# Modulation vectors: turning the four column quarters' sums with PE transposes and adding them on VectorE, in place of a float32 product with a folding matrix

## The chip, the core and the metric

The kernel runs on one core of one Trainium2 chip. The metric is the device time of one execution in microseconds (us); lower is better. The engines are named as the profile names them: PE is the matrix engine's matmul, PEld its weight load, DVE the vector engine, ACT the scalar engine, POOL the general engine, SP the engine whose queue issues nearly all DMAs.

## The reference, cut to what matters

The reference is one step of a two-layer decoder (layer 0 is RWKV-7, layer 1 sparse attention) for 1024 prompt tokens and for 8 sample sequences of 8 tokens. Every layer begins with its modulation vectors:

```
def ada_mods(c, w, b):
    m = jax.nn.silu(c) @ w + b
    return jnp.split(m[:, None, :], 6, axis=-1)
...
        sh_a, sc_a, g_a, sh_f, sc_f, g_f = ada_mods(c, P['w_ada'][i], P['b_ada'][i])
        h = rms_norm(x, P['norm_g'][i, 0]) * (1 + sc_a) + sh_a
        ...
        x = x + g_a * o
        h = rms_norm(x, P['norm_g'][i, 1]) * (1 + sc_f) + sh_f
        ...
        x = x + g_f * ((u * u) @ P['w_down'][i])
```

`c` has 9 rows (8 sample sequences and 1 prompt) of 1024 numbers, `w_ada[i]` is 1024 by 6144. So each layer turns 9 rows into 6 vectors of 1024 for each row: a product of few rows with a wide matrix. The rest of the step (projections, the RWKV recurrence, the choice of keys, attention, the feed-forward layers) is not touched by the change.

## The kernel before, in words

The activations lie with the 1024 model channels on partitions, as 8 blocks of 128. The large products (`mm3`, L140) split float32 operands into a high and a low part and add three products; their weights come through `loadw`, which splits them on ACT (L122) and on DVE or POOL (L126).

The modulation vectors are made in 24 steps of 256 columns for each of the two layers, 48 in all, by the generator `ada_steps`. `ada_prep` computes SiLU(c), turns it (L235) and keeps it in `cst`, 8 blocks of 128 channels by 32 columns, of which 9 hold rows and the others zero. A step does this:

- two loads of 512 KB of `w_ada` (L261, tile `wa`), each 4 blocks of 128 channels by 256 columns;
- eight float32 products (L264). The block k of a half (k = 0 to 3) writes output partitions 32k to 32k+31, so that the four blocks stand under each other in one PSUM tile `oa`; the second half is added to the first there. Thus `oa` holds four partial sums ("column quarters" of PE), each of 9 rows by 256 columns, at partitions 0, 32, 64 and 96;
- ACT copies `oa` to SBUF (L266, tile `adas`);
- `fold(s, sb)` then adds the four quarters and turns the result, so that the 256 columns come to lie on partitions as the activations' channels do. It is written one step late: the fold of step s-1 stands behind the products and the copy of step s. The product (L250) has the 128 by 128 half of `adas` as its stationary operand and a constant 128 by 10 matrix `fold` as the moving one, which has a 1 at row 32k + r, column r; so one product both turns and adds. DVE then adds the bias `b_ada` and writes the step's two columns of 128 channels by 9 rows into `mods` (L251).

The eight steps that layer 0's first norm needs run first (in `run`, with the load of the first group of tokens among them); `ada_fin` (L276) then makes `gm`, and `rwkv_h` applies `gm` and `mods` (L368, L371, L372). The other 40 steps are taken one at a time between the blocks of the RWKV projections of group A (64 sample columns and 512 prompt columns): `for _ in self.rwkv_proj(GA, hA): next(more, None)`. Those that are then left run one after the other. In this part the tiles `wa` have 3 buffers, the PSUM tiles `oa` and `pa` 2 each, `adas` 2. When the steps are done, their pools are closed, and the RWKV recurrence and group B's work begin.

Each engine works its own queue in order. The order in the queues is laid down when the program is built, and it is not always the order of the text.

Of the kernel before, what the change touches and what calls it, by code (L numbers as in the profile page):

```python
# [9 lines left out]
F32 = mybir.dt.float32  # L10
# [5 lines left out]
ALU = mybir.AluOpType  # L16
# [61 lines left out]
class Kern:  # L78
# [145 lines left out]
    def ada_prep(self):  # L224
        nc, cp = self.nc, self.cp
        c = self.quarter("c9", F32)[0:9].rearrange("p a b -> p (a b)")[:, 0:1024]
        nc.sync.dma_start(c[0:8], self.I["c_sample"])
        nc.sync.dma_start(c[8:9], self.I["c_prompt"])
        th = self.quarter("th9", F32)[0:9].rearrange("p a b -> p (a b)")[:, 0:1024]
        nc.scalar.activation(out=th, in_=c, func=AF.Tanh, scale=0.5)  # L230
        nc.vector.tensor_scalar(out=th, in0=th, scalar1=0.5, scalar2=0.5, op0=ALU.mult, op1=ALU.add)
        nc.vector.tensor_tensor(out=th, in0=th, in1=c, op=ALU.mult)
        o = self.mmt()
        for k in range(8):
            nc.tensor.transpose(o[:, k * 9:k * 9 + 9], th[:, k * 128:k * 128 + 128], self.ident[0:9, 0:9])  # L235
        self.cst = self.adp.tile([128, 8, 32], F32, name="cst")
        nc.vector.memset(self.cst, 0.0)
        nc.vector.tensor_copy(self.cst[:, :, 0:9], o[:, 0:72].rearrange("p (k r) -> p k r", k=8))
        self.mods = [cp.tile([128, 48, 9], F32, name=f"mods{l}") for l in range(2)]
        self.gm = [cp.tile([128, 2, 8, 9], F32, name=f"gm{l}") for l in range(2)]  # L240
        self.fold = self.adp.tile([128, 10], F32, name="fold")
        nc.sync.dma_start(self.fold, self.I["c_fold"])

    def ada_steps(self, l, s0, s1, pools):
        nc = self.nc

        def fold(s, sb):
            p = pools[1].tile([128, 512], F32, name="pa", tag="pa")
            for j in range(2):
                nc.tensor.matmul(p[:, j * 10:j * 10 + 10], sb[:, j * 128:j * 128 + 128], self.fold, start=True, stop=True)  # L250
            nc.vector.tensor_tensor(  # L251
                out=self.mods[l][:, s * 2:s * 2 + 2, :], in0=p[:, 0:20].rearrange("p (j r) -> p j r", j=2)[:, :, 0:9],
                in1=self.bada[:, l * 48 + s * 2:l * 48 + s * 2 + 2].unsqueeze(2).to_broadcast([128, 2, 9]), op=ALU.add)

        last = None
        for s in range(s0, s1):
            yield
            o = pools[1].tile([128, 512], F32, name="oa", tag="oa")
            for hf in range(2):
                w = pools[0].tile([128, 4, 256], F32, name="wa", tag="wa")  # L260
                nc.sync.dma_start(w, self.I["w_ada"][l, hf * 512:hf * 512 + 512, s * 256:s * 256 + 256].rearrange("(k p) f -> p k f", p=128))  # L261

                for k in range(4):
                    nc.tensor.matmul(o[k * 32:k * 32 + 32, 0:256], self.cst[:, hf * 4 + k, :], w[:, k, :], start=(hf == 0), stop=(hf == 1))  # L264
            sb = pools[2].tile([128, 256], F32, name="adas", tag="adas")
            nc.scalar.copy(sb, o[:, 0:256])  # L266
            if last:
                fold(*last)
            last = (s, sb)
        fold(*last)  # L270
# [1391 lines left out]
def consts():  # L1662
    c = {}
    c["c_ident"] = np.eye(128, dtype=np.float32)
    p = np.arange(128)
    s, t = p[:, None] % 64, np.arange(64)[None, :]
    strict, incl = (s < t), (s <= t)
    same = (s // 8) == (t // 8)
    gm = np.zeros((128, 2, 128), np.float16)
    gm[:, 0, :64], gm[:, 0, 64:] = strict, incl  # L1670
    gm[:, 1, :64], gm[:, 1, 64:] = strict & same, incl & same
    c["c_gmask"] = gm
    lm = np.zeros((128, 6, 128), np.float16)
    for i in range(6):
        m = 1 << i
        a, b = p[:, None], p[None, :]
        M = ((a // (2 * m)) == (b // (2 * m))) & ((a // m) % 2 == 1) & ((b // m) % 2 == 0)
        M = M | (a == b)
        lm[:, i, :] = M.T if i == 0 else M
    c["c_lmask"] = np.concatenate([lm[:64, :, :64], lm[64:, :, 64:]])  # L1680
    c["c_bones"] = ((p[:, None] // 64) == (p[None, :] // 64)).astype(np.float32)
    c["c_smask"] = ((p[:, None] % 64) // 8 == np.arange(8)[None, :]).astype(np.float32)
    rm = np.ones((128, 2, 256), np.float16)
    rm[:, 0, ::64] = 0
    rm[:, 1, ::8] = 0
    c["c_rmask"] = rm
    inv = np.float32(500000.0) ** (-np.arange(8, dtype=np.float32) * np.float32(2.0) / np.float32(16))
    rp = np.zeros((128, 9, 16), np.float32)
    for i in range(9):
        pos = (PAST + (p % 8) if i == 0 else (i - 1) * 128 + p).astype(np.float32)  # L1690
        ang = (pos[:, None] * inv[None, :]).astype(np.float32)
        rp[:, i, 0:8], rp[:, i, 8:16] = np.cos(ang), np.sin(ang)
    c["c_rope"] = rp
    c["c_cmask"] = np.where(p[None, :] <= p[:, None], 0, -3.0e38).astype(np.float32)
    c["c_csm"] = np.where(np.arange(8)[None, :] <= (np.arange(64)[:, None] % 8), 0, -3.0e38).astype(np.float32)
    c["c_qmask"] = (np.arange(8)[None, :] == (np.arange(128)[:, None] % 8)).astype(np.float32)
    c["c_iota16"] = (p[:, None] % 16).astype(np.float32)
    f = np.zeros((128, 10), np.float32)
    for r in range(128):
        if r % 32 < 9:  # L1700
            f[r, r % 32] = 1
    c["c_fold"] = f
    return c


# [40 lines left out]
```

## Time and profile before

| | us |
|---|---|
| median of 3 runs | 4280.88 |
| lowest, highest run | 4253.56, 4290.66 |
| profiled execution, its own time | 4286.67 |
| its span, first to last instruction | 4284.8 |
| mean granted PE clock in it | 0.915 of full speed |

The span is the stretch that all rows below are measured in; 1.9 us of the profiled execution's time lie around it. Busy shares are means over the whole span; the change touches only the first tenth of it.

### The profile page before, as it was taken

The numbers are of one execution on the slowest core, as the hardware profiler recorded it, in microseconds if no ns is written. First come the engines' busy times: TensorE is split into PE (matmuls) and PEld (weight loads), VectorE is DVE, ScalarE is ACT, GpSimd is POOL, SyncE is SP. The second block draws the span as 40 slices with busy tenths as digits, with TensorE's granted clock in tenths as the row PEclk, the third lists the DMA queues.
The fourth block names the chain that finished last, engine by engine and source line by source line (L and its number), as shares of the span: only waits on it lengthen the run. The fifth ranks groups of instructions, "written<-read, shape, count | busy, mean of one in ns | idle before, by whom it ended". The sixth has DMA issues, their size and how long they took to land.

```text
span 4284.8 us, 76620 instructions
## 1 busy us (share of the span) xinstructions
PE 3983.1 (93%) x31120; PEld 3196.4 (75%) x31120; DVE 2277.6 (53%) x5534; ACT 1688.9 (39%) x3147; POOL 964.0 (22%) x762
## 2 busy tenths in 40 slices
PE   7998899998999999989799888989988999999999
PEld 5787665666777799989655555778767777988777
DVE  5512775543667533341886954332899854444232
ACT  5632554433445333331454333332443334324332
POOL 1321321311433222212111122222101000222222
PEclk6798787978999999999799999998879999999999
DMA  6676122323322122234332156335211111323332
GB/s 217 203 235 210 51 71 71 95 56 99 111 60 61 46 76 81 83 111 123 118 95 65 50 177 209 120 122 152 91 41 46 45 40 45 118 89 96 94 94 84
DMA packets 555889, 433.84 MB, mean 101 GB/s; under 512 B 93777, under 2 KB 517313, under 8 KB 550354
## 3 DMA queue, kind: packets, MB, share of 16 engines
q1 hardware_dynamic: 549650, 391.20, 30.5%
q0 software_dynamic: 5888, 37.75, 2.5%
q8 instruction: 245, 4.01, 0.4%
q14 instruction: 106, 0.87, 0.1%
HBM read 360.48 MB, written 67.87 MB: 100 GB/s over the span
## 4 chain that ended last, share of the span: by engine, by line
PE 70%; DVE 14%; issue 6%; ACT 3%; DMA 3%; POOL 1%; SPq 0%; DVEq 0%; ACTq 0%; POOLq 0%
PE o L140 42%; DVE tj L1204 3%; PE o L1035 3%; PE po L1299 2%; PE pt L1293 2%; PE sp L1186 1%; PE gp L706 1%; PE tp L733 1%; DMA kvraw<-in_cache_k,ix 1%; PE sp L1185 1%; PE rb L659 1%; POOL wl L126 1%; PE sps L1509 1%; PE tp L754 1%; PE spn L930 1%
## 5 line engine op out<-in xcount | busy, mean ns | idle before, releaser
L126 POOL TENSOR_TENSOR wl<-w,wh 128x1024 fp32r<-128x1024 f32 (+1 forms) x258 | 612.0, 2373 | 2317.3 <-ACT wh L122 2038.6
L140 PE MATMUL o<-hi,wh 128*128 128x512 f32 (+4 forms) x2592 | 882.5, 345 | 21.9 <-ACT hi L144 21.8
L140 PE MATMUL o<-lo,wh 128*128 128x256 f32 (+4 forms) x2592 | 885.9, 343 | 16.4 <-DVE lo L145 11.9
L140 PE MATMUL o<-hi,wl 128*128 128x512 f32 (+4 forms) x2592 | 880.2, 340 | 0.1
L122 ACT CAST wh<-w 128x1024 fp32r<-128x1024 f32 (+3 forms) x388 | 401.3, 1034 | 998.6 <-PE o L140 906.1
L140 PEld LDWEIGHTS o<-hi,wh 128*128 128x128 f32 (+1 forms) x2592 | 498.2, 194 | 75.1 <-ACT hi L144 25.6
L140 PEld LDWEIGHTS o<-lo,wh 128*128 128x128 f32 (+1 forms) x2592 | 499.9, 193 | 70.1 <-DVE lo L145 16.3
L140 PEld LDWEIGHTS o<-hi,wl 128*128 128x128 f32 (+1 forms) x2592 | 498.6, 192 | 48.9 <-issue 11.1
L140 PE MATMUL o<-ul,wh 128*128 128x320 f32 (+2 forms) x1536 | 515.2, 336 | 20.8 <-DVE ul L145 20.7
L140 PE MATMUL o<-uh,wh 128*128 128x320 f32 (+2 forms) x1536 | 511.8, 336 | 2.1 <-DVE tno L1214 1.2
L140 PE MATMUL o<-uh,wl 128*128 128x320 f32 (+2 forms) x1536 | 512.6, 336 | 0.0
L397 DVE SCALAR_TENSOR_TENSOR xr<-o,mods,xr 128x256 f32<-128x256 f32 (+1 forms) x432 | 246.5, 571 | 320.4 <-PE o L140 319.5
L140 PEld LDWEIGHTS o<-ul,wh 128*128 128x128 f32 x1536 | 295.1, 192 | 51.3 <-DVE ul L145 28.3
L140 PEld LDWEIGHTS o<-uh,wh 128*128 128x128 f32 x1536 | 293.4, 192 | 35.1 <-ACT uh L144 8.1
L140 PEld LDWEIGHTS o<-uh,wl 128*128 128x128 f32 x1536 | 295.3, 192 | 25.0 <-issue 5.1
L145 DVE TENSOR_TENSOR ul<-z,uh 128x512 fp32r<-128x512 f32 (+1 forms) x128 | 129.7, 1014 | 319.0 <-ACT uh L144 318.9
L126 DVE TENSOR_TENSOR wl<-w,wh 128x1024 fp32r<-128x1024 f32 (+2 forms) x130 | 161.0, 1238 | 225.2 <-ACT wh L122 223.2
L1035 PE MATMUL o<-wl,hi 128*128 128x256 f32 (+2 forms) x648 | 188.0, 292 | 6.9 <-POOL wl L126 6.9
L1035 PE MATMUL o<-wh,hi 128*128 128x256 f32 (+2 forms) x648 | 187.1, 291 | 6.9 <-ACT hi L144 6.9
L1035 PE MATMUL o<-wh,lo 128*128 128x256 f32 (+2 forms) x648 | 183.9, 291 | 0.0
L1204 DVE TENSOR_SCALAR_CACHE_REDUCE tj<-sc,tcf 128x384 bf16<-128x384 f32 (+2 forms) x192 | 180.7, 941 | 2.8
L1276 ACT ACTIVATE sm<-sm,st 128x128 f32<-128x128 f32 (+7 forms) x128 | 99.3, 775 | 126.6 <-DVE st L1275 79.9
(415 smaller groups left out, 6838.7 us busy)
## 6 DMA issues: line engine op xcount, KB each, us to landing
w<-in_w_up SPq DMA_DIRECT2D x128, 512.0 KB
w<-in_w_down SPq DMA_DIRECT2D x128, 512.0 KB
wa<-in_w_ada SPq DMA_DIRECT2D x96, 512.0 KB
w<-in_rw_w_rkv SPq DMA_DIRECT2D x48, 512.0 KB
w<-in_att_w_in SPq DMA_DIRECT2D x32, 512.0 KB
RA<-pt SPq DMA_DIRECT2D x48, 288.0 KB
RB<-pt SPq DMA_DIRECT2D x48, 256.0 KB
in<-RA SPq DMA_DIRECT2D x32, 320.0 KB
```

Source lines behind the costliest of these rows:

```text
L122: nc.scalar.copy(h[:kp, :n], w[:kp, :n])
L126: eng.tensor_tensor(out=l[:kp, :n], in0=w[:kp, :n], in1=h[:kp, :n], op=ALU.subtract)
L140: nc.tensor.matmul(o[0:M, 0:c1 - c0], a, b[:, c0:c1], start=(i == 0 and q == 0), stop=(i == n - 1 and q == 2))
L145: (lo_eng or self.nc.vector).tensor_tensor(out=lo, in0=src, in1=hi, op=ALU.subtract)
L397: nc.vector.scalar_tensor_tensor(out=xm[:, p0:c1], in0=o[:, p0 - c0:c1 - c0], scalar=self.mods[l][:, j * 8 + m, 8:9], in1=xm[:, p0:c1], op ...
L659: nc.tensor.matmul(ps[half(h), i * n:i * n + n], y(i)[:, h:h + 1].to_broadcast([n, 64]), self.ident[0:n, 0:n], start=True, stop=True)
L706: nc.tensor.matmul(pvs[h][:, c, :], BK[hp, c].rearrange("p b t -> p (b t)")[:, h * 64:h * 64 + 128], AR[hp, c].rearrange("p b t -> p (b t) ...
L1035: nc.tensor.matmul(o[0:n, 0:cw], a, w, start=(k == 0 and q == 0), stop=(k == 7 and q == 2))
L1204: nc.vector.tensor_scalar(out=junk[:, 0:L], in0=s, scalar1=th if isinstance(th, float) else th[:, i:i + 1], scalar2=None, op0=op, op1=ALU. ...
L1276: nc.scalar.activation(out=sm[:, 0:L], in_=sm[:, 0:L], func=AF.Exp, scale=-1.0, bias=mn[:, 0:1], accum_out=sums)
L1293: nc.tensor.transpose(ps[:, jj * 128:jj * 128 + 128], sms[h + p][0][:, (j0 + jj) * 128:(j0 + jj) * 128 + 128], self.ident)
L1299: nc.tensor.matmul(out[gk][half(p), pr], self.V[:, j0 + jj, gk * 64:gk * 64 + 64], PTs[p][:, jj * 128:jj * 128 + 128], start=(j0 + jj == 0 ...
```

## The change

`fold` no longer multiplies with the folding matrix. PE turns each 128 by 128 half of `adas` with the identity that other transposes of the kernel use, into 128 PSUM columns each. A reduction on DVE then reads, for each of the two halves and 9 rows, the four quarters (32 columns apart) and adds them into `mods`. A second DVE instruction adds the bias in place. The constant `c_fold`, its tile and its load go.

```diff
@@ ada_prep
         self.gm = [cp.tile([128, 2, 8, 9], F32, name=f"gm{l}") for l in range(2)]
-        self.fold = self.adp.tile([128, 10], F32, name="fold")
-        nc.sync.dma_start(self.fold, self.I["c_fold"])
@@ ada_steps
         def fold(s, sb):
             p = pools[1].tile([128, 512], F32, name="pa", tag="pa")
             for j in range(2):
-                nc.tensor.matmul(p[:, j * 10:j * 10 + 10], sb[:, j * 128:j * 128 + 128], self.fold, start=True, stop=True)
+                nc.tensor.transpose(p[:, j * 128:j * 128 + 128], sb[:, j * 128:j * 128 + 128], self.ident)
+
+            m = self.mods[l][:, s * 2:s * 2 + 2, :]
+            nc.vector.tensor_reduce(out=m, in_=p[:, 0:256].rearrange("p (j k r) -> p j r k", j=2, k=4)[:, :, 0:9, :], axis=mybir.AxisListType.X, op=ALU.add)
             nc.vector.tensor_tensor(
-                out=self.mods[l][:, s * 2:s * 2 + 2, :], in0=p[:, 0:20].rearrange("p (j r) -> p j r", j=2)[:, :, 0:9],
+                out=m, in0=m,
                 in1=self.bada[:, l * 48 + s * 2:l * 48 + s * 2 + 2].unsqueeze(2).to_broadcast([128, 2, 9]), op=ALU.add)
@@ consts
-    f = np.zeros((128, 10), np.float32)
-    for r in range(128):
-        if r % 32 < 9:
-            f[r, r % 32] = 1
-    c["c_fold"] = f
```

## Rows read from the trace of the kernel before

**Rows 1.** The page: span, and busy time of each engine.
```profile
span 4284.8 us, 76620 instructions
...
PE 3983.1 (93%) x31120; PEld 3196.4 (75%) x31120; DVE 2277.6 (53%) x5534; ACT 1688.9 (39%) x3147; POOL 964.0 (22%) x762
```

**Rows 2.** Stretches of time: us, then busy us (count) of PE, PEld, DVE, ACT, POOL, clock, DMA.
```profile
130.00:152.00 22.00, 18.22 (x124) 14.16 (x124) 20.68 (x26) 17.00 (x31) 10.60 (x6) 0.98 0.60 192
152.00:188.00 36.00, 36.00 (x161) 24.18 (x159) 13.30 (x22) 15.83 (x29) 8.98 (x5) 0.54 0.45 149
...
204.00:247.00 43.00, 42.88 (x364) 38.98 (x363) 3.99 (x9) 13.52 (x26) 9.53 (x4) 1.00 0.86 268
```

**Rows 3.** Line L250, the product with the folding matrix: ns min/median/max, first and last start.
```profile
L250 PEld LDWEIGHTS pa<-fold,adas x192: 186/192/338, 11.3 to 408.6; 128*128 128x128 f32 x192
L250 PE MATMUL pa<-fold,adas x192: 172/258/387, 11.3 to 408.6; 128*128 128x10 f32 x192
```

**Rows 4.** The chain of waits, 0 to 412 us: shares by line, then start, us, what.
```profile
by line: PE o L140 42.3%; PE oa L264 7.0%; PE pa L250 4.0%; DMA wa<-in_w_ada 3.9%; PE o L605 2.4%; DVE xn L533 2.3%; issue 2.3%; ACT wh L122 1.5%; DMA w<-in_rw_w_rkv 0.9%; ACT ks L602 0.8%; DVE lo L145 0.8%; ACT hi L144 0.8%; DVE xn L531 0.
...
107.77 1.00 PE oa L264 x16
108.77 0.54 PE pa L250 x4
...
119.97 1.86 PE oa L264 x16
121.84 0.96 PE pa L250 x4
...
382.14 6.44 PE o L140 x48
...
389.58 0.54 PE pa L250 x4
...
390.97 6.05 DMA wa<-in_w_ada
...
408.06 0.95 PE pa L250 x4
```

**Rows 5.** The timeline of the first eight steps: start, us, engine, line.
```profile
26.58 0.93 PEld L250 LDWEIGHTS pa<-fold,adas 128*128 128x128 f32 x4 [1.35 <-ACT adas L266]
...
48.50 0.93 PEld L250 LDWEIGHTS pa<-fold,adas 128*128 128x128 f32 x4 [1.43 <-ACT adas L266]
...
49.78 0.23 DVE L276 SCALAR_TENSOR_TENSOR gm<-mods,vec 128x72 f32<-128x72 f32 x1
```

**Rows 6.** Transposes with the identity: line L307; runs of them in PE's timeline.
```profile
L307 PE MATMUL o<-c_ident,xr x72: 270/273/328, 3912.3 to 4278.7; 128*128 128x128 f32 x64, 128*64 128x128 f32 x8
...
4275.14 3.85 PE L307 MATMUL o<-c_ident,xr 128*128 128x128 f32 x32
...
410.51 1.97 PE L294 MATMUL o<-c_ident,xin 128*128 128x128 f32 x8
```

**Rows 7.** DVE operations nearest to the two of the change, by their shapes.
```profile
L1076 DVE TENSOR_REDUCE ss<-sq 128x1 f32<-128x64 f32 x8 | 1.7, 211 | 0.6 <-ACT sq L1075 0.6
L238 DVE COPY cst<-o x1: 234/234/234, 8.5 to 8.5; 128x72 f32<-128x72 f32 x1
L251 DVE TENSOR_TENSOR mods<-pa,vec 128x18 f32<-128x18 f32 x48 | 8.4, 175 | 142.4 <-PE pa L250 142.4
```

**Rows 8.** SP's queue near the start; ACT's order at the first steps.
```profile
1.88 0.36 SPq L242 DMA_DIRECT2D fold<-in_c_fold  x1
...
19.86 0.69 ACT L331 ACTIVATE acc<-x 128x576 f32<-128x576 f32 x1
...
23.58 0.37 ACT L266 COPY adas<-oa 128x256 f32<-128x256 f32 x1
```

**Rows 9.** The longest waits of 0 to 410 us: total, times, longest.
```profile
DVE mods L251 <- PE pa L250: 142.4, 40, 10.0
```

**Rows 10.** Transposes of the attention (L1293) in one stretch: busy PE, PEld, clock.
```profile
3500.00:3600.00 100.00, 19.47 (x119) 12.77 (x118) 1.00 0.15 43
```

## The prediction

> **What bounds the kernel now.** I read the page first: PE is busy 93% of a span of 4284.8 us and DVE 53% [rows 1]. That is a mean over stages, so I asked next where the changed lines run. The product with the folding matrix (L250) starts between 11.3 and 408.6 us and never after [rows 3]. The change can act only in the first tenth of the span; whatever it gains there reaches the end as a shift of everything behind it, if nothing behind it stands still.
>
> The table of stretches shows what kind of time that tenth is. In 204 to 247 us PE is busy 42.88 of 43.00 us, at full clock, with DVE nearly idle; in 152 to 188 us it is busy all the time at a granted clock of 0.54, that is mostly at the lower of its two levels; in 130 to 152 us DVE is the engine without a gap (20.68 of 22.00) [rows 2]. So most of the stretch is PE's own time, and a microsecond less of PE work is a microsecond, except around 130 to 152 us, where DVE is late, and where loads are late: the chain of waits has 3.9% of 412 us in loads of `w_ada`, the longest 6.05 us long [rows 4]. The chain gives the folding product 4.0% of 412 us, some 16 us [rows 4]. That is the ceiling for the part after 104 us (the chain cannot be followed further back than that; the first 50 us I read in the timeline).
>
> **The change part by part.**
>
> *PE, removed.* 48 folds of two products gave 192 weight loads and 192 matmuls [rows 3]: every float32 product runs as two pairs. A fold is thus four pairs, each a full 128-column weight load with 10 columns behind it, and the loads set its length: 0.54 us in the chain where the clock is high, 0.96 us where it is low [rows 4].
>
> *PE, added.* The transposes of line L307 are 72 in the text (nine blocks, two halves, four each) and 72 in the trace [rows 6], so a float32 transpose is one pair, not two. The data is again the stationary operand and now 128 identity columns follow instead of 10. At the end of the kernel 32 of them take 3.85 us with the tail of the last one (0.27 us) inside: (3.85 - 0.27) / 31 = 0.115 us apiece; at the low clock 8 take 1.97 us with a tail of 0.33 us (the longest of line L307): (1.97 - 0.33) / 7 = 0.23 us [rows 6]. Two of them: 0.23 us at the high clock, 0.46 us at the low one. A fold saves 0.54 - 0.23 = 0.31 us, or 0.96 - 0.46 = 0.50 us. Bounds: were two transposes as short as one pair of the old fold (0.54 / 4 = 0.13 us), 0.41 us at the high clock; were they to run as two passes each, nothing.
>
> *Where these lie on the path.* (a) The first eight steps: from 26.58 to 48.50 us the timeline has six folds at the low clock, each behind the copy that it or its neighbour waits for and each with PE's next products right behind it [rows 5], and one at the high clock before them: 6 x 0.50 + 0.31 = 3.3 us. The fold at 11.26 us lies ahead of a wait for loads and counts nothing. (b) 104 to 204 us: of the chain's 26 fold pieces two high ones and five low ones lie here, the first at 108.77 and at 121.84 us: 2 x 0.31 + 5 x 0.50 = 3.1 us. A short third piece at 128.41 us ends on DVE and gains nothing, since DVE gets more to do there. (c) 204 to 391 us: 14 whole high pieces, the last at 389.58 us [rows 4], 14 x 0.31 = 4.3 us, and two cut ones, 0.3 us. The folds here that are no pieces of the chain run while ACT prepares the next block, and count nothing. (d) 391 to 412 us: PE waits for loads [rows 4], but the loads are issued when the products behind a fold have freed a buffer, so the chain runs through two low folds, the last at 408.06 us [rows 4]: 1.0 us. Of the folds between 51 and 104 us, which the chain doesn't show, I take none. Sum: 3.3 + 3.1 + 4.6 + 1.0 = 12.0 us.
>
> *DVE, added.* A reduction of 72 numbers from PSUM into 18, and the addition now follows it. The reduction of 64 numbers takes 211 ns and a copy of 72 numbers from PSUM 234 ns; the addition took 175 ns and will again [rows 7]. I take 0.23 us a step, 11 us in all, in a stretch where DVE is idle in most parts: it stood 142.4 us in 40 waits for the fold itself [rows 9], so the reduction begins where that wait ended and the next DVE work is late by 0.25 us at most. What hides this is that DVE is not last; without that cover it is all 11 us. Who waits for `mods`: `gm`, once, after the eighth step [rows 5], and the work behind the last step: 2 x 0.25 = 0.5 us on the path. The chain has no fold in DVE's full stretch (130 to 152 us), only the one just ahead. Bound: were all ten pairs between 104 and 204 us on DVE's path, 2.3 us.
>
> *The constant and its load.* One issue of 0.36 us leaves SP's queue at 1.88 us [rows 8], and all later loads are issued that much sooner. The first thing that PE and ACT wait for is `c`, issued before it, so I count nothing; if the loads of the first steps were the only limit, 0.36 us. PSUM: `pa` keeps its size and its two buffers; 256 of its columns are written instead of 20.
>
> *Sum.* 12.0 - 0.5 = 11.5 us less. Against the profiled execution: 4286.7 - 11.5 = 4275.2 (span 4273.3). That execution lies 5.8 us above the median of the runs, so for a median I take 4280.9 - 11.5 = 4269. The three runs lie 37 us apart, and 1% of the time (43 us) is about what a measurement of this kernel can tell from no change: the forecast is well below that.
>
> **The rivals.**
>
> *Given back.* The time is saved but a later wait takes it: loads of `w_ada` that PE already waits for (the 6.05 us at 390.97, [rows 4]) land when the memory delivers them, not when PE is ready. If all that (b) to (d) gain is lost so, only (a) stays: -3 us, 4278. For it: DMA is busy 0.86 of 204 to 247 us [rows 2]. Against it: in that very stretch PE has no gap, so the loads come in time.
>
> *The queues' order, to the bad.* The order in the queues is not that of the text: ACT's squares of the norm (L331), written behind all eight steps, run at 19.86 us, before the second step's copy at 23.58 [rows 8]. With other instructions the build may lay them otherwise. The place where it would hurt is DVE's queue, which stands at the head of a fold for up to 10.0 us [rows 9]; today this hides, as DVE has nothing urgent behind it. If a pair is laid ahead of the splits that feed PE's next projection, PE stands as long. There are three such changes of projection between 128 and 251 us: 3 x 10 = 30 us, less the 11.5 gained: 4299. It decides as soon as more than 11.5 us of such waits come onto PE's path. For it: nothing in the trace fixes the order. Against: the change alters two instructions of a step, and where it moves queues the waits can as well get shorter.
>
> *The order, to the good.* The same, with waits that go. PE's gap in DVE's full stretch is 22.0 - 18.2 = 3.8 us [rows 2] and the loads' part of the chain is 3.9% of 412, 16 us [rows 4]: all of it and the forecast's 11.5 are 31 us, 4250.
>
> *The clock.* Between the folds of 204 to 391 us the granted clock is full [rows 2]; L264's sixteen pieces take 1.00 us there and 1.86 us at the low level [rows 4]. A transpose that let the clock fall would cost the block behind it: 6.44 us of products [rows 4] would take up to 1.86 times as long, 5.5 us more; on 14 folds 77 us, less 11.5: 4346. The trace speaks against it: in 3500 to 3600 us, 119 transposes lie between products and the granted clock is 1.00 [rows 10]. The Trainium skill (TensorE: Matmul & The Clock Gate, Part 4: PE-mode transpose) speaks against the change here: it says that transposes don't count as busy time in the same way and that the full clock doesn't engage for them. By that rule this rival would be the forecast; the stretch at 3500 us, with its clock of 1.00, doesn't agree with it for transposes mixed with products.
>
> *It doesn't do what it says.* If this transpose runs as two passes, like a product, four pairs with 128 columns replace four with 10: nothing gained, DVE's 0.5 us lost, 4281. Line L307's count speaks against it.
>
> **How the numbers follow.** Forecast 0.56 (its own range 4250 to 4284, from the runs' spread around it); given back 0.14; order to the bad 0.12; order to the good 0.12; clock 0.03; two passes 0.03. The likeliest gives 4269. The range must leave out no more than 2 in 10: it takes in both order rivals, with the runs' spread a little beyond them, 4232 to 4300, and leaves out the clock. Faster by over 1% (under 4238): a third of the good order and a little of the forecast's spread, 0.07; slower by over 1% (over 4324): the clock and the worst of the bad order, 0.05; within 1%: 0.88.
>
> **What would show it.** In the changed kernel's profile: 96 transposes with 96 weight loads in place of 192 and 192; fold pieces of about 0.22 and 0.40 us in the chain; a reduction of some 0.23 us for each step on DVE; `gm` made near 46.7 us rather than 49.78; the last fold near 397 us rather than 408, and everything behind it in the same order and as long as before. Wrong would be: PE's gaps before 412 us grown by more than PE's work shrank (given back), queues in another order with DVE waits on PE's path (order), a lower granted clock in 204 to 391 us (clock), or the time behind 412 us changed by more than a few us, which none of my steps foresees.

## The result, and the profile after

The changed kernel takes 4231.45 us (median of 4 runs, 4227.15 to 4245.93) against 4279.41 us before (4 runs beside it), a ratio of 0.990 with a 95% interval of 0.986 to 0.994. It is faster, by some 43 us by the ratio and 48 us by the medians; the forecast was 11.5 us. (The ratios here leave out runs that lie over 1.5% above their kernel's fastest, so they can differ a little from the medians.) The profiled execution took 4245.93 us, the slowest of the four. In the changed kernel the lines behind `fold` stand one higher than before: L265 is the old L264, and so on.

The operations first. By source line (ns min/median/max, first and last start), the transposes, the reduction, the addition; then the addition by its shape with its mean:

```profile
L248 PEld LDWEIGHTS pa<-c_ident,adas x96: 137/142/230, 11.6 to 391.2; 128*128 128x128 f32 x96
L248 PE MATMUL pa<-c_ident,adas x96: 271/328/477, 11.6 to 391.4; 128*128 128x128 f32 x96
...
L251 DVE TENSOR_REDUCE mods<-pa x48: 217/232/234, 12.3 to 391.8; 128x18 f32<-128x72 f32 x48
L252 DVE TENSOR_TENSOR mods<-mods,vec x48: 158/179/1861, 13.3 to 392.6; 128x18 f32<-128x18 f32 x48
...
L252 DVE TENSOR_TENSOR mods<-mods,vec 128x18 f32<-128x18 f32 x48 | 29.3, 612 | 1.2
```

96 pairs stand where 192 stood [rows 3], and the reduction takes the 0.23 us of the forecast. The addition doesn't take what was forecast: its median is 179 ns, but it now has a mean of 612 ns and a longest of 1861, where the old one had a mean of 175 [rows 7]. The timeline (start, us) shows what it stands beside when it is long:

```profile
201.59 2.40 POOL L126 TENSOR_TENSOR wl<-w,wh 128x1024 fp32r<-128x1024 f32 x1 [5.35 <-PE oa L265]
201.91 0.23 DVE L251 TENSOR_REDUCE mods<-pa 128x18 f32<-128x72 f32 x1 [5.64 <-PE pa L248]
202.18 1.84 DVE L252 TENSOR_TENSOR mods<-mods,vec 128x18 f32<-128x18 f32 x1
```

POOL's split began at 201.59 and ends at 203.99; the addition begins inside it and ends with it, at 204.02. The reduction inside the same split is not stretched. The whole timeline bears this out: 18 of the 48 additions take over 0.3 us, and each of the 18 overlaps an instruction of POOL and ends within 0.04 us of that instruction's end. In the kernel before 25 additions overlap one too, and none takes over 0.18 us:

```profile
L251 DVE TENSOR_TENSOR mods<-pa,vec x48: 164/177/178, 13.3 to 409.0; 128x18 f32<-128x18 f32 x48
```

Now the stages, by the columns of [rows 2]. Before, from `gm` to the steps' last product, and from there to the last L605 (a small product at the end of group B's key projection):

```profile
49.80:406.80 357.00, 332.90 (x2439) 275.99 (x2439) 130.05 (x263) 163.03 (x301) 90.83 (x48) 0.85 0.66 212
406.80:1042.10 635.30, 577.70 (x5935) 393.36 (x5927) 354.27 (x977) 280.77 (x623) 162.99 (x209) 0.78 0.26 71
```

and the same two stretches of the changed kernel, with its 20 to 50 us ahead of them:

```profile
20.00:50.00 30.00, 17.11 (x155) 9.30 (x155) 19.58 (x86) 14.07 (x28) 0.00 (x0) 0.82 0.97 317
...
43.50:389.90 346.40, 318.71 (x2351) 259.39 (x2355) 157.07 (x299) 161.71 (x299) 91.83 (x48) 0.87 0.71 221
389.90:998.50 608.60, 550.27 (x5981) 376.67 (x5973) 356.79 (x984) 281.66 (x626) 163.20 (x209) 0.83 0.27 74
```

So the lead is 6.3 us at `gm` (43.5 against 49.8), 16.9 us at the last product, 43.6 us at the last L605; 34.5 us at the last update of the recurrence's state, 1467.5 against 1502.0, in these rows of the kernel before and of the changed one:

```profile
L921 DVE SCALAR_TENSOR_TENSOR S<-S,EL,spn x128: 268/276/283, 472.3 to 1502.0; 128x64 f32<-128x64 f32 x128
```
```profile
L922 DVE SCALAR_TENSOR_TENSOR S<-S,EL,spn x128: 268/276/282, 450.8 to 1467.5; 128x64 f32<-128x64 f32 x128
```

At the end it is 41.0 us (spans 4284.8 and 4243.8). More than half of the lead is made behind 393 us, where no instruction of the change runs. In that stretch the granted clock is 0.83 instead of 0.78. The granted clock has two levels, 1 and a half, so this is some 0.34 x 609 = 207 us at the low one instead of 0.44 x 635 = 280.

What differs there is the order of the queues. With the steps' own instructions left out, the two built programs have the same instructions, but about one in eight of PE's stands in another order than before. All of these lie behind the steps and before 1500 us; from there on all queues are the same.

### The profile page after: what moved, and what is told of

Its sections match the earlier page's. It is cut to its first block, busy times and chain, and to the rows that moved or that the text cites. A ratio compares the mean times of both kernels' runs of the same rounds, so it can differ in the third digit from the quotient of the medians.

```text
span 4243.8 us, 76490 instructions
## 1 busy us (share of the span) xinstructions
PE 3933.9 (93%) x31024; PEld 3154.4 (74%) x31024; DVE 2310.4 (54%) x5582; ACT 1690.0 (40%) x3147; POOL 963.7 (23%) x762
## 4 chain that ended last, share of the span: by engine, by line
PE 54%; DVE 12%; issue 5%; DMA 2%; ACT 2%; POOL 1%; SPq 0%; DVEq 0%; ACTq 0%; POOLq 0%
PE o L140 34%; DVE tj L1205 4%; PE o L1036 3%; PE po L1300 2%; PE pt L1294 2%; PE sp L1187 1%; DMA kvraw<-in_cache_k,ix 1%; PE sp L1186 1%; POOL wl L126 1%; PE gp L707 1%; DVE ul L145 1%; PE ip L1187 1%; PE sps L1510 1%; PE tp L734 1%; DVE xr L398 1%
## 5 line engine op out<-in xcount | busy, mean ns | idle before, releaser
L140 PE MATMUL o<-hi,wh 128*128 128x256 f32 (+4 forms) x2592 | 883.2, 345 | 18.1 <-ACT hi L144 17.5
L140 PE MATMUL o<-hi,wl 128*128 128x256 f32 (+4 forms) x2592 | 879.8, 340 | 0.7 <-POOL wl L126 0.7
L140 PE MATMUL o<-ul,wh 128*128 128x320 f32 (+2 forms) x1536 | 513.4, 335 | 20.9 <-DVE ul L145 20.7
```

The lines of the kernel that those rows point to most:

```text
L140: nc.tensor.matmul(o[0:M, 0:c1 - c0], a, b[:, c0:c1], start=(i == 0 and q == 0), stop=(i == n - 1 and q == 2))
```

## Experiments

Twelve measurements were made, of eleven kernels, each beside the kernel before. Two theories were to be told apart. *Theory W*: the shorter folds, and what they do to PE's clock, give the gain. *Theory O*: half comes from the queues' other order, which the build lays down when the steps at the end have other instructions. In the built programs the order behind 412 us depends on the last steps alone: if the last eight steps of layer 1 are the old ones, it is the order of before, whatever the 40 others are, and if they are the new ones, it is that of the changed kernel. PE's queue, the steps left out, is exactly one of the two in seven of the eleven programs, and differs from one of them in fewer than ten places in the other four. That gives each order with either kind of fold. Within theory W two readings are kept apart: *theory P*, that a fold's number of pairs and their length count, and *theory C*, that the transposes' 128 columns bring PE's clock up by themselves. In the edits below, words in capitals stand for code that is cut short. Each `gm`, last product and last L605 is that of one profiled execution, set against the one profile of the kernel before; that execution (4286.7 us) is some 16 us longer than the medians of the later runs of the same kernel (4269.7 to 4270.9), so the differences of whole times decide.

**40 new folds, old order** (`last8_old`). `fold` is written with both ways, chosen by step:

```diff
-            for j in range(2): OLD PRODUCT
+            new = not (l == 1 and s >= 16)
+            for j in range(2): TRANSPOSE if new else OLD PRODUCT
+            if new: REDUCE
+            ADD BIAS IN PLACE if new else OLD ADDITION
```

> 40 of the 48 steps fold by transposes, the last eight of layer 1 by the old product. The queues behind 412 us are then laid as in the kernel before. Theory W (the shorter folds and PE's clock before 412 us give the gain, which is then only carried to the end): nearly the whole gain stays, 35 to 43 us under before, the last fold some 15 us sooner than 408 us, and the lead grows behind it as in the changed kernel. Theory O (some 15 us are gained before 412 us and the rest by the other order of the queues between 412 and 1500 us): the last fold is some 15 us sooner, the lead stays at that size to the end, 12 to 20 us under before.

Measured: 4242.0 us (median of the ten runs that the ratio keeps; 4245.5 of all twelve) against 4270.1, -28.1 us, 0.992 (0.988 to 0.996). Its stretches from `gm` and from the last product:

```profile
44.60:374.50 329.90, 299.23 (x2375) 247.10 (x2377) 157.05 (x295) 160.90 (x301) 90.80 (x48) 0.94 0.72 230
374.50:1029.70 655.20, 595.96 (x5934) 404.75 (x5927) 355.48 (x977) 282.02 (x623) 163.71 (x209) 0.76 0.25 68
```

The lead of this execution is 32.3 us at the last product and only 12.4 us at the last L605: against the kernel before the clock was higher in the first stretch (0.94 and 0.85) and lower in the second (0.76 and 0.78). The runs' -28.1 lies between the two theories, so by itself it settles nothing.

**8 new folds, new order** (`last8_new`). The same with `new = l == 1 and s >= 16`.

> Only the last eight steps of layer 1 fold by transposes, the 40 others by the old product. The queues behind 412 us are then laid as in the changed kernel. Theory W: next to nothing of the work is changed, 0 to 6 us under before. Theory O: little before 412 us (0 to 4 us), then a lead of 17 us or more that appears between 412 and 1500 us, 15 to 28 us under before in all.

Measured: 4246.2 us against 4270.1, -23.9 us, 0.996 (0.993 to 0.998).

```profile
50.90:401.90 351.00, 325.19 (x2418) 267.57 (x2418) 131.11 (x269) 161.62 (x299) 90.80 (x48) 0.87 0.68 215
401.90:999.70 597.80, 538.16 (x5980) 368.34 (x5973) 356.14 (x984) 281.58 (x626) 162.96 (x209) 0.85 0.27 75
```

With 40 of 48 folds as before, the lead is 4.9 us at the last product and 42.4 us at the last L605. The runs' 23.9 us (18 by the ratio) is theory O's number and not W's (0 to 6 us): the order alone is worth some 20 us. The lead of 42.4 us in this one profile is no proof of it, as the next experiment but one shows.

**Only the first eight steps new** (`first8_new`; `new = l == 0 and s < 8`), order of before.

> Only the eight first steps of layer 0 fold by transposes; the order of all queues but for four DVE instructions is that of before. If the transposes themselves bring PE's clock up in the first 50 us (theory C), the factors gm are ready near 43.5 us as in the changed kernel, at a granted clock over 0.8 in 20 to 50 us. If the clock's rise there was chance, gm is ready near 46.7 us with the shorter folds alone, at a clock near 0.58. Whole time 3 to 7 us under before, or the same within its interval.

Measured: 4263.6 us against 4270.1, -6.5 us, 1.000 (0.997 to 1.003): the same. `gm` came at 43.6 us in the profile, at a clock of 0.82 in 20 to 50 us, as theory C says. One execution was not enough for that, as the next but one shows. In this profile the last product came at 385.4 us, 21.4 us sooner than before's, with eight folds of 48 changed and no gain that the runs show. So the time of the last product in one profile doesn't measure the folds either.

```profile
385.40:1011.50 626.10, 567.49 (x5935) 387.89 (x5927) 353.80 (x977) 280.38 (x623) 163.05 (x209) 0.80 0.26 72
```

**One pass, 10 columns** (`one_pass`). The tiles `adas` and `fold` become fp32r, with a cast of the matrix (`fold`'s lines are left out here); order of before.

```diff
-            sb = pools[2].tile([128, 256], F32, name="adas", tag="adas")
+            sb = pools[2].tile([128, 256], F32R, name="adas", tag="adas")
```

> The old product with 10 columns, but in the reduced float32 form (fp32r) of the large products: the sums and the folding matrix are rounded to it, so that a fold needs two pairs instead of four, with one DVE instruction as before and the order of before. If fewer pairs are what pays, it is as good before 412 us as the transposes: gm near 46 us and the last fold 12 to 17 us sooner. Theory C (the transposes' 128 columns bring the clock up) says that with 10 columns the clock stays near 0.58 in 20 to 50 us and that less is gained: gm not before 46 us, the last fold 8 to 12 us sooner. Whole time by theory O 8 to 17 us under before.

Measured: 4246.0 us against 4270.1, -24.1 us, 0.995 (0.993 to 0.998): nearly what the 40 transposed steps give in the same order, with one DVE instruction and 10 columns. `gm` came at 45.0 us and the last product 11.6 us sooner. In this order, then, two pairs in place of four are enough for the gain, without transposes. The lead at the last L605 is 35.0 us here, with the order of before: a single profile's lead there doesn't tell the two orders apart.

```profile
395.20:1007.10 611.90, 552.32 (x5932) 375.90 (x5925) 354.26 (x977) 279.90 (x623) 163.81 (x209) 0.82 0.27 73
```

**The changed kernel again** (`changed_again`), written in as many lines as before.

> The changed kernel itself, with as many lines as before, on one chip with the next three. If half of its gain is the shorter fold and half the order of the queues behind it: 30 to 48 us under before, gm ready at 43 to 45 us, the last product of the steps at 375 to 392 us, and 1063 to 1075 us from there to the end of the recurrence (L921), as in the two kernels with this order so far.

Measured: 4230.3 us against 4270.9, -40.6 us, 0.993 (0.990 to 0.995). But `gm` came at 48.6 us in this execution, not 43.5, with the clock at the low level for most of 20 to 50 us as before; the last product came 13.4 us sooner than before's, the last L605 39.9 us. So the clock's early rise in the first profile was one execution's. The stretch of 20 to 50 us of the kernel before and of this execution, then this execution's two stretches:

```profile
20.00:50.00 30.00, 23.96 (x165) 14.66 (x166) 14.88 (x47) 8.13 (x18) 0.00 (x0) 0.58 0.90 319
```
```profile
20.00:50.00 30.00, 22.55 (x157) 11.00 (x154) 17.01 (x60) 9.62 (x21) 0.00 (x0) 0.59 0.97 319
```

```profile
48.60:393.40 344.80, 318.01 (x2348) 258.73 (x2351) 157.81 (x301) 161.72 (x299) 91.48 (x48) 0.87 0.71 219
393.40:1002.20 608.80, 550.29 (x5981) 376.57 (x5973) 356.52 (x984) 281.69 (x626) 163.24 (x209) 0.83 0.27 74
```

**The second DVE instruction alone** (`dve_twice`), order of before:

```diff
-            nc.vector.tensor_tensor(out=m, in0=SUMS IN PSUM, in1=BIAS, op=ALU.add)
+            nc.vector.tensor_copy(m, SUMS IN PSUM)
+            nc.vector.tensor_tensor(out=m, in0=m, in1=BIAS, op=ALU.add)
```

> The old product on PE, and the change's second DVE instruction alone: the sums are copied from PSUM to mods (48 copies of 18 numbers), then the bias is added in place. The order of before. If DVE's added time is covered, as forecast, the time is that of before within 5 us, gm near 50 us, the last products near 402 to 407 us. If it is on the path, up to 8 us over before, the last products later by as much.

Measured: 4278.0 us against 4270.9, +7.2 us, 1.003 (1.001 to 1.006). The copy from PSUM is short, the addition from SBUF is again long:

```profile
L252 DVE TENSOR_TENSOR mods<-mods,vec 128x18 f32<-128x18 f32 x48 | 29.7, 619 | 1.1
L251 DVE COPY mods<-pa 128x18 f32<-128x18 f32 x48 | 8.3, 174 | 134.0 <-PE pa L250 134.0
```

In its profile the last product came 1.9 us later than before's. The interval (3 to 24 us) leaves out zero, so the instruction is not wholly covered, but the runs don't give its size.

```profile
408.70:1036.30 627.60, 568.74 (x5935) 387.36 (x5927) 354.15 (x978) 280.62 (x623) 163.34 (x209) 0.80 0.26 72
```

**Turned twice** (`turned_twice`): `for j in (0, 1, 0, 1): TRANSPOSE`, new order but for a few places.

> Each half is turned twice into the same columns, so that a fold has four pairs again, of 128 columns each, as long as the old one; the queues are laid as in the changed kernel but for a few places. If only the number of pairs pays before 412 us (theory P): gm at 49 to 51 us, the last products at 400 to 407 us, and 12 to 22 us under before from the order alone. If columns that keep PE busy bring the clock up (theory C): gm at 43 to 46 us though the folds are as long, the last products before 396 us, 25 us or more under before.

Measured: 4231.7 us against 4270.9, -39.1 us, 0.992 (0.989 to 0.995), as quick as the changed kernel, with twice its pairs. `gm` at 47.7 us, the last product at 378.7, clock 0.96 in between. The fold is not quite as long as the old one, though: its four weight loads take 0.42 us where the clock is high, the old ones 0.52.

```profile
47.70:378.70 331.00, 302.19 (x2426) 250.13 (x2425) 155.37 (x299) 160.78 (x299) 91.42 (x48) 0.96 0.72 228
378.70:1002.10 623.40, 562.31 (x5983) 383.90 (x5975) 356.60 (x984) 281.70 (x626) 163.22 (x209) 0.81 0.26 72
```

**A folding matrix of 128 columns** (`wide_product`), 118 of them zero, in the old product; new order but for a few places.

> The old product with a folding matrix of 128 columns, of which 118 are zero: four pairs of 128 columns, the quarters still added by PE, one DVE instruction as before, the queues laid as in the changed kernel but for a few places. Theory P: as turned_twice, gm at 49 to 51 us, 12 to 22 us under before by the order. Theory C: gm at 43 to 46 us and 25 us or more under before. If the order gives nothing: not under before at all by P.

Measured: 4245.2 us against 4270.9, -25.7 us, 0.995 (0.992 to 0.998). `gm` came at 49.1 us, as theory P says; the gain lies above P's 12 to 22 us, at the edge of theory C's. The order alone (`last8_new`) gives as much.

```profile
396.10:994.90 598.80, 539.32 (x5983) 369.06 (x5975) 355.35 (x983) 281.41 (x626) 162.83 (x209) 0.85 0.27 75
```

**Filled, 40 steps** (`filled_40`). Work is added to the kernel before, in its own order but for a few places:

```diff
             for j in range(2): OLD PRODUCT
+            for j in range(2 if (l == 0 or s < 16) else 0):
+                nc.tensor.transpose(p[:, 128 + j * 128:256 + j * 128], sb[:, j * 128:j * 128 + 128], self.ident)
```

> The kernel before with work added: in the first 40 of the 48 steps, behind the old product, PE also turns both halves of adas into columns of pa that nobody reads (80 transposes, some 9 to 18 us of PE time). The queues are otherwise laid as before. If it is work alone that counts: 6 to 15 us over before, the last products at 412 to 420 us. If PE's columns bring the clock up (theory C): the time at the low clock between gm and the last products falls from some 104 us to under 75, the last products come no later than 407 us, and the whole is not over before.

Measured: 4272.1 us against 4269.7, +2.4 us, 1.002 (0.999 to 1.004).

```profile
54.90:392.30 337.40, 312.27 (x2500) 261.69 (x2503) 133.30 (x263) 161.28 (x301) 91.99 (x48) 0.95 0.71 224
392.30:1037.60 645.30, 586.44 (x5935) 398.18 (x5927) 355.45 (x977) 281.78 (x623) 163.66 (x209) 0.76 0.25 70
```

In the profile the last product comes 14.5 us sooner in spite of 80 transposes more (clock 0.95 from `gm` on), and at the last L605 only 4.5 us are left. The runs show no gain; their median is under the 6 to 15 us that the work alone would cost, but the interval (-3 to +19 us) takes these in.

**Filled, all steps** (`filled_all`), new order but for a few places:

> The same in all 48 steps; the queues behind 412 us are then laid as in the changed kernel. Work alone and no effect of the order: 8 to 18 us over before. Order alone (as in last8_new, 18 to 24 us under), less the added work: 5 to 15 us under before. Order and theory C together: 20 us or more under before, and less than 90 us at the low clock between gm and the last products.

Measured: 4253.3 us against 4269.7, -16.4 us, 0.996 (0.994 to 0.999). From `gm` to the last product 357.0 us at 0.88, as long as before; the gain appears behind it:

```profile
406.40:1009.00 602.60, 542.79 (x5985) 372.20 (x5977) 355.89 (x983) 281.72 (x626) 162.82 (x209) 0.85 0.27 74
```

**The bias once for each group of steps** (`bias_once`), new order:

```diff
-            nc.vector.tensor_tensor(out=m, in0=m, in1=BIAS OF THE STEP, op=ALU.add)
...
         fold(*last)
+        m = self.mods[l][:, s0 * 2:s1 * 2, :]
+        nc.vector.tensor_tensor(out=m, in0=m, in1=BIAS OF ALL ITS STEPS, op=ALU.add)
```

> The changed kernel without the second DVE instruction of each step: the reductions write mods, and the bias is added once for each group of steps (three instructions of 72 to 432 numbers in place of 48 of 18). Queues as in the changed kernel. If the second DVE instruction was covered, as forecast: the same as the changed kernel within 4 us, some 40 us under before. If it costs what dve_twice showed (7 us over before): 45 us or more under before, which would beat both kernels.

Measured: 4225.1 us (4211.5 to 4230.2, 6 runs) against 4269.7, -44.6 us, 0.990 (0.987 to 0.993). It beats the kernel before. Against the changed kernel (0.993 and 0.990 in its two measurements) it is at most a few us better, which the intervals don't separate.

```profile
373.80:985.70 611.90, 553.99 (x5981) 377.02 (x5973) 357.31 (x986) 281.53 (x626) 162.92 (x209) 0.82 0.27 73
```

**The first experiment again** (`last8_old_2`).

> last8_old again, to tell what of it was chance: 41 us at the low clock before its last products, 321 us between there and the last L605. If the low clock's shares are the kernel's own: 35 to 50 and 300 to 340 us again. If they are drawn in each execution: 60 to 100 us and 215 to 275 us, as in the other kernels with before's order. Whole time in either case 18 to 35 us under before; at less than 12 us the shorter folds alone would give next to nothing.

Measured: 4239.9 us against 4269.7, -29.7 us, 0.992 (0.989 to 0.995). The same program shows quite another clock:

```profile
48.60:395.30 346.70, 319.71 (x2371) 262.49 (x2372) 157.11 (x294) 162.61 (x301) 91.43 (x48) 0.87 0.69 218
395.30:1035.70 640.40, 580.79 (x5934) 395.65 (x5927) 354.95 (x977) 281.12 (x623) 163.38 (x209) 0.78 0.26 70
```

0.87 and 0.78 where it had 0.94 and 0.76. In the first stretch the share at the low clock is drawn in each execution, then; in the second it is low for the old order both times.

**Taken together.** The medians against before, in us: 40 new folds with the old order -28.1 and -29.7; 40 old folds with the new order -23.9; both -40.6 and, in the first measurement, -48. So each half is measured alone. Whether they add up in full is not shown: their sum is 52 to 54 us, and the intervals are 10 to 16 us wide to either side. Put otherwise, the folds give 28 to 30 us in the old order and 16 in the new one (4246.2 to 4230.3), the order 24 us with old folds and 10 to 12 with new ones. Two more pairs show the order with like folds: `last8_new` against `first8_new`, eight new folds each, 17 us, and `filled_all` against `filled_40`, 19 us.

What the order does is seen when the kernels are sorted by the stretch from the last product to the last L605, with the time at the low clock worked out as above (twice what the clock lacks to 1, times the length):

| order, kernel | length, us | clock | at the low clock, us |
|---|---|---|---|
| old: one_pass | 612 | 0.82 | 220 |
| old: first8_new | 626 | 0.80 | 250 |
| old: dve_twice | 628 | 0.80 | 251 |
| old: before | 635 | 0.78 | 280 |
| old: last8_old_2 | 640 | 0.78 | 282 |
| old: filled_40 | 645 | 0.76 | 310 |
| old: last8_old | 655 | 0.76 | 314 |
| new: last8_new | 598 | 0.85 | 179 |
| new: wide_product | 599 | 0.85 | 180 |
| new: filled_all | 603 | 0.85 | 181 |
| new: changed, and again | 609, 609 | 0.83 | 207 |
| new: bias_once | 612 | 0.82 | 220 |
| new: turned_twice | 623 | 0.81 | 237 |

All lie near one line, some 0.42 us of length for each us at the low clock ((655 - 598) / (314 - 179)), and where an old and a new one have the same low time (220 us) they have the same length. Waits don't make the difference: the length less PE's busy time, PE's idle time, is 57.6 to 61.1 us in all fourteen profiles. So the new order neither shortens the work there nor its waits; PE runs less at the low clock, 202 us on average against 272, and 71 x 0.42 is 30 us. A part of that is lost again behind the last L605: at the last update of the state the two averages are 1468 and 1489 us, 21 us apart, near what the runs show for the order.

The table holds one thing more. In the new order the stretch is the longer the sooner it begins: 612 and 623 us where the last product came before 380 us, 609 twice at 390 and 393, 598 to 603 at 396 to 406. So at the last L605 the changed kernel (998.5 and 1002.2 us) is no further than `last8_new` (999.7), which has 40 old folds: in these profiles the clock has taken back what the folds gained. Where the 16 us lie by which the changed kernel's runs are the quicker, the profiles don't show.

## Why the prediction was right in sign and a quarter of the size

It said 4269, in 4232 to 4300, most likely within 1%; measured were 4231.5, half a us under the range's lower edge, and 1.0% under the kernel before. The sign held, and so did the mechanism of the sum as far as it can be tested; what the sum left out was the larger part. That the left-out part helped and did not hurt is luck.

- *PE removed and added.* 96 pairs for 192, as counted. At the high clock, one step of 204 to 391 us followed the other after 240.84 - 232.85 = 7.99 us before and 232.56 - 224.80 = 7.76 us after: 0.23 us a step, not 0.31, so this term was a quarter too large. These are the rows of before and after from which that is read:

```profile
232.85 0.52 PEld L250 LDWEIGHTS pa<-fold,adas 128*128 128x128 f32 x4 [0.41 <-issue]
240.84 0.52 PEld L250 LDWEIGHTS pa<-fold,adas 128*128 128x128 f32 x4 [0.41 <-issue]
```
```profile
224.80 0.20 PEld L248 LDWEIGHTS pa<-c_ident,adas 128*128 128x128 f32 x2 [0.41 <-issue]
232.56 0.20 PEld L248 LDWEIGHTS pa<-c_ident,adas 128*128 128x128 f32 x2 [0.41 <-issue]
```

- *Terms (a) to (d)*, 11.5 us up to the last product: 16.9 us in the first profile, 13.4 us in the second. Term (a), 3.3 us, was 6.3 and 1.2 us, with the clock of 20 to 50 us as the difference (0.82 and 0.59; before 0.58). That agrees with the sum but doesn't test it: the same program reached its last product at 374.5 us in one execution and at 395.3 in another (`last8_old`).
- *DVE added.* The size was wrong: 11 us of DVE work were forecast, measured are 11.0 us of reductions and 29.3 - 8.4 = 20.9 us more for the additions. The step that failed is "the addition took 175 ns and will again": it read PSUM and SBUF, and now reads two operands in SBUF, as POOL's split does. Where it stands alone (`dve_twice`) it costs 7 us of the time by the medians, 3 to 24 by the interval, and not 0.5.
- *"Everything behind it in the same order and as long as before"* is the step that failed most: the other order behind 412 us, to which the sum gave nothing, is worth 10 to 24 us. The queues' other order was a rival at 0.12, worked out as 31 us to the good, 4250, out of waits of DVE and loads before 412 us. It came true with another place and another mechanism: behind the last product, through the clock. Its sign could not have been told from the trace of before, and no row shows why PE's clock is higher in this order.
- *Given back* did happen in some profiles, behind the last product and through the clock, not through loads: `last8_old` lost 20 of its 32 us there, `filled_40` 10 of its 14.5, and the new order's kernels what "Taken together" says. `one_pass` and `first8_new` lost nothing there.
- *The clock's fall* did not come: in the changed kernel the clock is 0.87 from `gm` to the last product, against 0.85. (The full clock that the prediction reads for 204 to 391 us stands in [rows 2] for 204 to 247 alone; over the whole of it the trace has 0.99.) With `filled_40`'s 80 transposes more than before it was 0.95. The Trainium skill (TensorE: Matmul & The Clock Gate, Part 4: PE-mode transpose) says that the full clock doesn't engage for transposes; with these float32 transposes between products no fall is seen, and no run here has a long stretch of transposes alone.
- *Two passes* is ruled out by the 96 pairs.

Open stays why this order keeps PE's clock higher, and whether the transposes' 128 columns bring the clock up by themselves (theory C). `turned_twice` (-39.1 us with four pairs, if somewhat shorter ones) and perhaps `filled_40` speak for it; `wide_product` and `filled_all`, which gain what the order gives or less, speak against. The clock of a single profile decides nothing here, as `last8_old`'s two executions show.

## What to carry to other kernels

Where a build lays the queues' order, a small local edit can relay everything behind it, so an edit should be tried with both orders before its gain is put down to it; here the edit's work is worth 16 to 30 us and the accident of the order 10 to 24. A float32 product pays each of its weight loads twice, which is most of it where few columns follow; a transpose, or a product in one pass, pays it once. When an operand moves from PSUM to SBUF, the new DVE instruction has to be costed beside what POOL does at the time, not by its own length.

## What the runs showed of the hardware that was not expected

A DVE addition of 18 numbers with two SBUF operands took 0.18 us (median) and up to 1.86 us beside POOL's splits, ending with the split (202.18 us in the changed kernel), while a reduction from PSUM beside the same split took its usual 0.23 us. The Trainium skill (SBUF — State Buffer, SBUF: two separate sides) says that a DVE instruction with two SBUF inputs and a POOL instruction that reads SBUF share a pair of ports, which the one that starts first holds for its whole instruction; the trace agrees, as all 18 long additions end with an instruction of POOL. The weight load of 128 columns takes 142 ns (median) in front of a transpose and 192 ns in front of a float32 product [rows 3]. And the same program (`last8_old`) drew a clock of 0.94 in one execution and 0.87 in another over the same work, which took 330 and 347 us.
